# Hybrid attention decoder layer: where the tiles begin in SBUF

## The chip, the cores and the metric

The kernel runs on one NeuronCore of a Trainium2 chip, as one launch. The metric is the device time of that launch in microseconds (us). Three runs of the kernel before took 886.53, 885.81 and 889.96 us; the median is 886.53 us.

## What is computed

One decoder layer for 512 tokens of 1024 channels, in float32. One input projection feeds two causal mixers: a sparse attention of eight heads with three branches (compressed, selected, window) and a gated DeltaNet of four heads in chunks. Their outputs are projected, gated, merged and projected again, then normed; a gated MLP with a short convolution follows. Cut to its frame:

```python
h = x @ w_in                                   # 1024 -> 5408
y_a = nsa_attention(...) @ w_nsa_out           # 512 -> 1024
y_b = gated_deltanet(...) @ w_gdn_out          # 512 -> 1024
mix = (sigmoid(gate_a) * y_a + sigmoid(gate_b) * y_b) @ w_o
x = layer_norm(ALPHA * x + mix, ln1_g, ln1_b)
h = causal_dwconv(x @ ffn_w_up, ffn_conv_w)    # 1024 -> 5632
gate, val = split(h, 2)
f = (silu(gate) * val) @ ffn_w_down            # 2816 -> 1024
x = layer_norm(ALPHA * x + f, ln2_g, ln2_b)
```

## The kernel before

**The products.** Each large product is done in three passes of float32r parts. Both operands are split into a high part (a float32r copy) and a low part (the rest), and `product` (L192) adds high by high, high by low and low by high in one PSUM bank:

```python
PE.matmul(ps, wh[k], mh_(k), start=(k == 0), stop=False)
PE.matmul(ps, wh[k], ml_(k), start=False, stop=False)
PE.matmul(ps, wl[k], mh_(k), start=False, stop=(k == n - 1))
```

The first operand is stationary: 128 columns of it are loaded into TensorE before each matmul (LDWEIGHTS, shown as PEld). The second is moving: 512 columns of it, 2048 bytes of each partition, stream through. A matmul and the weight load of the next one overlap, so both read SBUF at once.

**The stages.** All work is issued through a tile framework that sets the order by priorities (a written-out `ORDER`, with a shift for each step) and the waits by the tiles' places.

- Phase one, up to about 376 us: the token-major projection (`pb`), then the channel-major input projections (`gemm_t` L205, tiles `gps`: weights `wh`/`wl` stationary, `xh`/`xl` moving), interleaved with both mixers. The mixers' own products are small: scores (`aps`), values (`pout` L773: `vcat` stationary, `pth`/`ptl` moving, 256 columns), and many float32 products and transposes (`dps`) of the DeltaNet.
- Merge, about 376 to 464 us (L832 to L872): the outputs are split into `yoh` (high) and `yol` (low); each step does some gate projections (`gps`, as above) and then the mixers' output projections (`pm`: `wh`/`wl` stationary, `yoh`/`yol` moving).
- w_o and the first norm, about 464 to 511 us (L923 to L941, `pw`): here `mh`/`ml` are stationary and `woh`/`wol` move; the normed rows are transposed back into `mh`/`ml`.
- Up product, about 511 to 758 us (L949 to L995, `pu`): `wh`/`wl` stationary, `mh`/`ml` moving; the first two pairs of units run by halves of 256 columns (L958 to L964). The convolution and the gate run beside it on VectorE, ScalarE and GpSimd and write `ah`/`al`.
- Down product, about 758 to 879 us (L1000 to L1027, `pdn`): `ah`/`al` stationary, the streamed `wh`/`wl` moving; the last eight blocks of the second half have their weights kept in tiles of their own, `th`/`tl` (L1012 to L1020), so that each token tile ends in turn. The second norm follows and the rows go out.

**The places.** A pool takes a stretch of each partition's bytes; pools stack from the left end up or from the right end down, and a pool closed gives its stretch to the next one. A tile begins where the tiles before it in its pool end, rounded up to 32 bytes. Nothing else in the program fixes an address. On the left the constants' pool (`cp`, L143) holds 512, 32 and 528 bytes, so the pool `stream` (`wp`, L144: `raw`, `wh`, `wl`, all of 2048 or 4096 bytes) and all that stacks on it (`xh`, `xl`, `yol`, `x1`, `ah`, `al`) begin 192 bytes past a multiple of 256. On the right the stack starts 32 bytes below a multiple of 256, and `mh`, `ml`, `yoh`, `woh`, `wol`, `th`, `tl` begin 224 past one. In phase one the small tiles of `nsa` and `slots` (16 to 384 bytes, L150 and L151) stand among the large ones and shift them.

Of the kernel before, what the change touches and what calls it, by code (L numbers as in the profile page):

```python
# [10 lines left out]
F32 = mybir.dt.float32  # L11
# [119 lines left out]
def body(ctx: ExitStack, tc: tile.TileContext, d, out):  # L131
# [1 line left out]
    V, A, G, PE = nc.vector, nc.scalar, nc.gpsimd, nc.tensor  # L133

    def E(name, h, d="V"):
        """The engine of a step in its h-th turn."""
        return {"V": V, "G": G, "A": A}[ENGINE.get(f"{name}{h}", d)]

    def bc(ap, shape):
        return ap.to_broadcast(shape)  # L140

    psum = lambda name, bufs: ctx.enter_context(tc.tile_pool(name=name, bufs=bufs, space=PSUM))
    cp = ctx.enter_context(tc.tile_pool(name="consts", bufs=1))  # L143
    wp = ctx.enter_context(tc.tile_pool(name="stream", bufs=2))  # L144

    early = ExitStack()
    pool = lambda st, **kw: st.enter_context(tc.tile_pool(**kw))
    xp = pool(early, name="xp", bufs=1, side="left")
    ph1 = ExitStack()
    nsa = pool(ph1, name="nsa", bufs=1, side="right")  # L150
    sp = pool(ph1, name="slots", bufs=1, side="right")  # L151
    def slot(tag, name, shape=(128, 512), dt=F32):
        return sp.tile(list(shape), dt, name=name, tag=tag, bufs=BUFS[tag])

# [5 lines left out]
    dps = lambda shape=(128, 512): pd.tile(list(shape), F32, name="dps")  # L160
    aps = lambda shape=(128, 512): pa.tile(list(shape), F32, name="aps")

    # ---------------------------------------------------------------- loads
    xh = xp.tile([128, KD, S], F32R, name="xh")
    xl = xp.tile([128, KD, S], F32R, name="xl")

# [4 lines left out]
        V.tensor_tensor(xl[:, k, :], xr, xh[:, k, :].bitcast(F32), op=OP.subtract)  # L171

    def split_w(src, shape, eng, first=A):
        """The rows of a unit as two float32r parts, in two halves along its first free dimension."""
        raw = wp.tile(shape, F32, name="raw", bufs=BUFS["raw"])
        nc.sync.dma_start(out=raw, in_=src)
        half = shape[1] // 2
        hi, lo = [], []
        for i in range(2):
            r = raw[:, i * half:(i + 1) * half]  # L180
            wh = wp.tile([128, half] + list(shape[2:]), F32R, name="wh", bufs=BUFS["wh"])
            if first is A:
                A.activation(wh, r, AF.Copy)  # L183
            else:
                first.tensor_copy(wh, r)
            wl = wp.tile([128, half] + list(shape[2:]), F32R, name="wl", bufs=BUFS["wl"])
            eng.tensor_tensor(wl, r, wh.bitcast(F32), op=OP.subtract)  # L187
            hi += [wh[:, k] for k in range(half)]
            lo += [wl[:, k] for k in range(half)]
        return hi, lo  # L190

    def product(ps, w, m, n):  # L192
        """Three passes of float32r parts, w stationary, over n blocks of the contraction."""
        (wh, wl), (mh_, ml_) = w, m
        first = None
        for k in range(n):
            i = PE.matmul(ps, wh[k], mh_(k), start=(k == 0), stop=False)  # L197
            first = first or i
            PE.matmul(ps, wh[k], ml_(k), start=False, stop=False)  # L199
            PE.matmul(ps, wl[k], mh_(k), start=False, stop=(k == n - 1))  # L200
        return first
# [12 lines left out]
    def rsqrt(o, i, n):  # L214
        G.tensor_tensor(o, i, minus_half[:, :n], op=OP.pow)  # L215

    # -------------------------------------------- token-major projections
    vcat = nsa.tile([128, TT, 2, 2, 2, 64], F32R, name="vcat")
    gsig = nsa.tile([128, TT, 24], F32, name="gsig")
    bd = nsa.tile([128, TT, 8], F32, name="bd")  # L220
# [56 lines left out]
    gdt = rows("gdt", d["gdt"], 4)  # L277


    # decay and beta of all heads: [token in chunk, chunk, head]  # L280
    hbeta = nsa.tile([128, TT, GH], F32, name="hbeta")
    beta = nsa.tile([128, TT, GH], F32, name="beta")
    gdec = nsa.tile([128, TT, GH], F32, name="gdec")
# [39 lines left out]
        A.activation(eg.rearrange("p a b c -> p (a b c)"), ps[:, :48], AF.Exp)  # L323
        V.scalar_tensor_tensor(nbe, beta, -1.0, eg[:, 0], op0=OP.mult, op1=OP.mult)

    # ----------------------------------------------------------- GDN
    yo_tile = lambda name, dt=F32: yo.tile([128, S], dt, name=name, tag="yo", bufs=9)
    yT, oT = [None] * GH, [None] * GH

# [34 lines left out]
            e.tensor_tensor(o, i, bc(f, c4), op=OP.mult)  # L364

    def norms(h, i, ps):
        """Reciprocal lengths over the channels of ps: [token, chunk, channel]."""
        ss = sp.tile([128, TT], F32, name="ss", bufs=2)
        rn = sp.tile([128, TT], F32, name=f"rn{i}", bufs=2)
        junk = sp.tile([128, 128], F32, name="junk", bufs=1)  # L370
        for c in range(TT):
            A.activation(junk, ps[:, c, :], AF.Square, accum_out=ss[:, c:c + 1])
        V.tensor_scalar(ss, ss, 4.0 * RMS_EPS, None, op0=OP.add)
        rsqrt(rn, ss, TT)
        return rn
# [65 lines left out]
    def gdn_tri(h):  # L441
        st = HS[h]
        m = st["m"]
        # 16 x 16 diagonal blocks by substitution
        lo = slot("mid", "lo", c4)
        E("lo", h).tensor_tensor(lo, m, bc(C["low"][:, None, :], c4), op=OP.mult)
        f16 = sp.tile([128, TT, 16], F32, name="f16", bufs=2)
# [133 lines left out]
        yT[h] = yo_tile("yT")  # L581
        V.scalar_tensor_tensor(yT[h], py.rearrange("p a b -> p (a b)"), gnw, gs, op0=OP.mult, op1=OP.mult)

    # ----------------------------------------------------------- NSA
    KK = {}

    def keys(g):
        """Keys of one group, of the selected and the window branch, each part twice over the partitions."""
        ps = gemm_t(18 + g, after=HOLD.get("k") if g else None)
        hh_ = nsa.tile([128, 2, S], F32R, name="kh")  # L590
        ll_ = nsa.tile([128, 2, S], F32R, name="kl")
        KK[g] = (hh_, ll_)
        for br in range(2):
            hh, ll = hh_[:, br], ll_[:, br]
            own, oth = slice(br * 64, br * 64 + 64), slice(64 - br * 64, 128 - br * 64)
            for rows_ in (own, oth):
                A.activation(hh[rows_], ps[own], AF.Copy)
            for rows_ in (own, oth):
                V.tensor_tensor(ll[rows_], ps[own], hh[own].bitcast(F32), op=OP.subtract)  # L599
# [113 lines left out]
    POUT = {}  # L713

    def scores(h, u):
        """Exponentials of one or two query tiles, scaled by gate over sum: [query, branch, key]."""
        g = h // 4
        slope = 2.0 ** -(h + 1)
        parts = UNITS[u]
        w = 512 // len(parts)  # L720
        ps = aps((128, len(parts), w))
        s = slot("att", "sc", (128, len(parts), w))
        mn = nsa.tile([128, 3, len(parts)], F32, name="mn", bufs=3)
        br, t = parts[0]
        n = (t + 1) * 128
        brs, ts = slice(br, br + len(parts)), slice(t * 128, n)
        PE.matmul(ps[:, :, :n], Q2[h][:, ts], KK[g][0][:, brs, :n], start=True, stop=False)
        HOLD["k"] = HOLD[h] = PE.matmul(ps[:, :, :n], Q2[h][:, ts], KK[g][1][:, brs, :n], start=False, stop=True)
        for i, (br, t) in enumerate(parts):
            n = (t + 1) * 128  # L730
            V.tensor_tensor_reduce(out=s[:, i, :n], in0=ps[:, i, :n], in1=C["alibi"][:, 512 - n:], scale=-slope,  # L731
                                   scalar=3.0e38, op0=OP.add, op1=OP.min, accum_out=mn[:, 0, i:i + 1])
            A.activation(s[:, i, :n], s[:, i, :n], AF.Exp, scale=-1.0, bias=mn[:, 0, i:i + 1],  # L733
                         accum_out=mn[:, 1, i:i + 1])
        V.reciprocal(mn[:, 2, :], mn[:, 1, :])
        for i, (br, t) in enumerate(parts):
            n = (t + 1) * 128
            e = E(f"p{u}", h)
            sc = gsig[:, t, (br + 1) * 8 + h:(br + 1) * 8 + h + 1]
            if e is A:  # L740
                V.tensor_tensor(mn[:, 2, i:i + 1], mn[:, 2, i:i + 1], sc, op=OP.mult)
                A.activation(s[:, i, :n], s[:, i, :n], AF.Copy, scale=mn[:, 2, i:i + 1])
            else:
                e.tensor_scalar(s[:, i, :n], s[:, i, :n], mn[:, 2, i:i + 1], sc, op0=OP.mult, op1=OP.mult)
        return s

    def flip(h, u, s):
        """Their transposes as two parts, and the products with the values once a half is whole."""
        g = h // 4
        parts = UNITS[u]  # L750
        br, t = parts[0]
# [53 lines left out]
        A.activation(t, ps, AF.Tanh, scale=0.5)  # L805
        MG[i] = t

    # --------------------------------------------------- order of phase one
    pd = ps1.enter_context(tc.tile_pool(name="pd", bufs=BUFS["pd"], space=PSUM))
    pa = ps1.enter_context(tc.tile_pool(name="pa", bufs=BUFS["pa"], space=PSUM))  # L810
    po = ps1.enter_context(tc.tile_pool(name="po", bufs=1, space=PSUM))
# [16 lines left out]
    ph1.close()  # L828
    ps1.close()

    # ------------------------------------------------------------- merge
    mix = ExitStack()  # L832
    mx = pool(mix, name="mx", bufs=1, side="right")
    mh = mx.tile([128, KD, S], F32R, name="mh")
# [39 lines left out]
    early.close()  # L874
    ps2.close()

    # ------------------------------------------------- w_o and first norm
    ln = ctx.enter_context(tc.tile_pool(name="ln", bufs=1, side="left"))
    x1 = ln.tile([128, TT, D], F32, name="x1")
    ln2 = ln.tile([128, 2, D], F32, name="ln2")  # L880
    fs = ctx.enter_context(tc.tile_pool(name="fs", bufs=1, side="left"))
# [8 lines left out]
    rows_of(ln1, 0)  # L890

    def layer_norm(r, gb, st, after=lambda i: None):
        """r: the rows' values, normed in place by halves; st: their two bn_stats."""
        mv = ln.tile([128, 2], F32, name="mv", bufs=2)
        V.bn_aggr(out=mv, in_=st)
        rs = ln.tile([128, 1], F32, name="rs", bufs=2)
        V.tensor_scalar(rs, mv[:, 1:2], LN_EPS, None, op0=OP.add)  # L897
        rsqrt(rs, rs, 1)
        for i in range(2):
            cs = slice(i * 512, (i + 1) * 512)  # L900
            V.scalar_tensor_tensor(r[:, cs], r[:, cs], mv[:, 0:1], gb[:, 0, cs], op0=OP.subtract, op1=OP.mult)
            V.scalar_tensor_tensor(r[:, cs], r[:, cs], rs, gb[:, 1, cs], op0=OP.mult, op1=OP.add)
            after(i)
# [37 lines left out]
        layer_norm(r, ln1, st)  # L941
    wos.close()

    # --------------------------------------------------------------- FFN
    NE = 2
    fws = ExitStack()
    fw = pool(fws, name="fw", bufs=1, side="left")
# [111 lines left out]
```

## Time and profile before

| what | value |
|---|---|
| median of three runs | 886.53 us |
| lowest and highest | 885.81 and 889.96 us |
| span of the profiled execution | 886.6 us |
| TensorE busy (matmul) | 856.7 us, 97% |
| VectorE busy | 563.9 us, 64% |
| ScalarE busy | 384.9 us, 43% |
| GpSimd busy | 159.3 us, 18% |
| bytes moved | 76.33 MB |

The profiled execution's own time stands here as its span, 886.6 us; no time around it is shown. The page counts a matmul as busy from its start to a modelled end, and matmuls overlap, so the busy share does not tell how closely they follow each other. That is read from the timeline, where the first number of a row is the start in us from the beginning of the span.

### The profile page before, as it was taken

What the parts mean: (1) busy time and instruction counts of PE and PEld (TensorE: products, weight loads), DVE (VectorE), ACT (ScalarE), POOL (GpSimd) and SP (SyncE); (2) the same over time, 40 slices, a digit from 0 to 9 for tenths busy, and PEclk for the clock granted to TensorE, in tenths of its full rate; (3) what the DMA queues carried; (4) which work ended last, traced back from release to release, by engine and by line L of the source; (5) the groups of instructions that cost most, each with busy time, mean ns of one, the idle gap of its engine ahead of it and who ended that gap; (6) DMA issues with size and microseconds to landing.
All of it is one profiled execution on the core that took longest, in us unless ns stands there. A gap on an engine that the chain in (4) does not pass through costs nothing.

```text
span 886.6 us, 11725 instructions
## 1 busy us (share of the span) xinstructions
PE 856.7 (97%) x4292; PEld 698.9 (79%) x4292; DVE 563.9 (64%) x1159; ACT 384.9 (43%) x855; POOL 159.3 (18%) x141
## 2 busy tenths in 40 slices
PE   9899799989899899999999999999999999999996
PEld 8677687767787678888888898888888888888885
DVE  5755769985856976585457646666666666423337
ACT  5463267567356666542234114444444444322220
POOL 1232342324334220111100001111111111000001
PEclk9999799999989999999999999999999999999999
DMA  8322111101211010254356002222222222333222
GB/s 265 94 76 91 48 48 36 37 25 48 61 36 48 25 48 25 72 167 152 122 178 237 24 1 72 96 95 94 93 90 93 91 93 93 102 105 97 97 72 95
DMA packets 22954, 76.33 MB, mean 86 GB/s; under 512 B 3184, under 2 KB 3568, under 8 KB 22640
## 3 DMA queue, kind: packets, MB, share of 16 engines
q1 hardware_dynamic: 22896, 75.57, 25.9%
q8 instruction: 34, 0.56, 0.3%
q14 instruction: 24, 0.20, 0.1%
HBM read 73.47 MB, written 2.10 MB: 85 GB/s over the span
## 4 chain that ended last, share of the span: by engine, by line
PE 86%; DVE 9%; ACT 3%; issue 1%; DMA 1%; POOL 0%; SPq 0%; DVEq 0%; ACTq 0%; POOLq 0%
PE pu L200 9%; PE pu L197 9%; PE pu L199 9%; PE gps L197 7%; PE gps L200 7%; PE gps L199 7%; PE pdn L1003 5%; PE pdn L1004 5%; PE pdn L1002 5%; PE pout L773 2%; PE pm L197 2%; DVE tmp L463 2%; PE pm L200 2%; PE pm L199 2%; PE pw L936 2%; PE pw L938 2%
## 5 line engine op out<-in xcount | busy, mean ns | idle before, releaser
L187 DVE TENSOR_TENSOR wl<-raw,wh 128x512 fp32r<-128x512 f32 (+1 forms) x172 | 134.1, 781 | 142.3 <-ACT wh L183 139.3
L183 ACT ACTIVATE wh<-raw 128x512 fp32r<-128x512 f32 (+1 forms) x198 | 122.6, 622 | 234.2 <-PE pu L199 107.5
L197 PE MATMUL pu<-mh,wh 128*128 128x512 f32 (+1 forms) x384 | 144.3, 376 | 0.0
L199 PE MATMUL pu<-ml,wh 128*128 128x512 f32 (+1 forms) x384 | 144.3, 376 | 0.0
L200 PE MATMUL pu<-mh,wl 128*128 128x512 f32 (+1 forms) x384 | 144.3, 376 | 0.0
L197 PE MATMUL gps<-xh,wh 128*128 128x512 f32 x320 | 131.4, 411 | 1.0 <-DVE kl L599 0.6
L200 PE MATMUL gps<-xh,wl 128*128 128x512 f32 x320 | 130.5, 408 | 0.0
L199 PE MATMUL gps<-xl,wh 128*128 128x512 f32 x320 | 129.2, 404 | 0.0
L187 POOL TENSOR_TENSOR wl<-raw,wh 128x512 fp32r<-128x512 f32 x48 | 63.5, 1325 | 171.8 <-ACT wh L183 107.0
L200 PEld LDWEIGHTS pu<-mh,wl 128*128 128x128 f32 x384 | 72.0, 187 | 14.8
L199 PEld LDWEIGHTS pu<-ml,wh 128*128 128x128 f32 x384 | 72.0, 188 | 14.7
L197 PEld LDWEIGHTS pu<-mh,wh 128*128 128x128 f32 x384 | 72.0, 187 | 14.6
L987 DVE SCALAR_TENSOR_TENSOR fa<-pu,fcw,fa 128x511 f32<-128x511 f32 x88 | 65.7, 746 | 10.3 <-ACT fa L984 8.8
L197 PEld LDWEIGHTS gps<-xh,wh 128*128 128x128 f32 x320 | 61.1, 191 | 13.1 <-issue 1.5
L200 PEld LDWEIGHTS gps<-xh,wl 128*128 128x128 f32 x320 | 61.2, 191 | 11.2 <-POOL wl L187 0.3
L199 PEld LDWEIGHTS gps<-xl,wh 128*128 128x128 f32 x320 | 61.2, 191 | 10.6 <-issue 0.4
L993 POOL TENSOR_TENSOR fth<-fth,fa 128x512 f32<-128x512 f32 x22 | 28.7, 1304 | 219.7 <-DVE fa L987 219.7
L1003 PE MATMUL pdn<-wl,ah 128*128 128x512 f32 x144 | 56.0, 389 | 0.0
L1002 PE MATMUL pdn<-wh,ah 128*128 128x512 f32 x144 | 56.0, 389 | 0.0
L1004 PE MATMUL pdn<-wh,al 128*128 128x512 f32 x144 | 56.0, 389 | 0.0
L733 ACT ACTIVATE sc<-sc,mn 128x384 f32<-128x384 f32 (+2 forms) x64 | 35.7, 558 | 15.0 <-DVE mn L731 14.3
L215 POOL TENSOR_TENSOR rs<-rs,minus_half 128x1 f32<-128x1 f32 x8 | 7.5, 941 | 185.7 <-DVE rs L897 185.7
(295 smaller groups left out, 1543.3 us busy)
## 6 DMA issues: line engine op xcount, KB each, us to landing
raw<-in_up SPq DMA_DIRECT2D x44, 512.0 KB, 3.6
raw<-in_wT SPq DMA_DIRECT2D x40, 512.0 KB, 3.6
raw<-in_down SPq DMA_DIRECT2D x22, 512.0 KB, 3.4
raw<-in_wm SPq DMA_DIRECT2D x8, 512.0 KB, 3.6
raw<-in_wo SPq DMA_DIRECT2D x8, 512.0 KB, 3.5
xr<-in_xT SPq DMA_DIRECT2D x8, 256.0 KB, 4.7
ln<-in_lnr SPq DMA_DIRECT2D x2, 1024.0 KB, 6.5
xax<-in_x SPq DMA_DIRECT2D x4, 512.0 KB, 5.2
```

Of the source, the lines that this page charges most:

```text
L183: A.activation(wh, r, AF.Copy)
L187: eng.tensor_tensor(wl, r, wh.bitcast(F32), op=OP.subtract)
L197: i = PE.matmul(ps, wh[k], mh_(k), start=(k == 0), stop=False)
L199: PE.matmul(ps, wh[k], ml_(k), start=False, stop=False)
L200: PE.matmul(ps, wl[k], mh_(k), start=False, stop=(k == n - 1))
L463: V.tensor_tensor(tmp[:, :, :n], lx[:, :, r + 1:, r], bc(xs[:, :, r:r + 1], (128, TT, n)), op=OP.mult)
L733: A.activation(s[:, i, :n], s[:, i, :n], AF.Exp, scale=-1.0, bias=mn[:, 0, i:i + 1], accum_out=mn[:, 1, i:i + 1])
L987: V.scalar_tensor_tensor(acc[:, n:], ps[:, :S - n], w[:, i:i + 1], acc[:, n:], op0=OP.mult, op1=OP.add)
L993: G.tensor_tensor(th, th, g[1], op=OP.mult)
L1002: PE.matmul(ps, ah[:, k, ts], wh, start=(k == 0), stop=False)
L1003: PE.matmul(ps, ah[:, k, ts], wl, start=False, stop=False)
L1004: PE.matmul(ps, al[:, k, ts], wh, start=False, stop=(k == NF - 1))
```

## The change

A helper class `Rows` takes the place of three pools of phase one and of the pool of the norms. It keeps two pools: one for tiles whose bytes in a partition are a multiple of 256, and one (its name ends in `_s`) for all others; at the end it fills the second up to a multiple of 256. At both ends of SBUF a tile of its own (128 bytes left, 224 right) moves the start of the stack to a multiple of 256. All sizes, loops, engines and priorities stay.

```diff
+    class Rows:
+        def __init__(self, st, name, bufs, **kw):
+            self.small = st.enter_context(tc.tile_pool(name=name + "_s", bufs=bufs, **kw))
+            st.callback(self.fill)
+            self.big = st.enter_context(tc.tile_pool(name=name, bufs=bufs, **kw))
+            self.bufs, self.used = bufs, {}
+        def tile(self, shape, dt, name, tag=None, bufs=None):
...
+            n = 4 * math.prod(shape[1:])
+            if n % 256 == 0:
+                return self.big.tile(list(shape), dt, **kw)
+            n, m = -(-n // 32) * 32, bufs or self.bufs
+            self.used[tag or name] = max(n * m, self.used.get(tag or name, 0))
+            return self.small.tile(list(shape), dt, **kw)
+        def fill(self):
+            left = -sum(self.used.values()) % 256
+            if left:
+                self.small.tile([128, left // 4], F32, name="rest")
...
-    cp = ctx.enter_context(tc.tile_pool(name="consts", bufs=1))
+    for side, n in (("left", 128), ("right", 224)):
+        edge = ctx.enter_context(tc.tile_pool(name="edge_" + side, bufs=1, side=side))
+        edge.tile([128, n // 4], F32, name="edge_" + side)
+    cp = Rows(ctx, "consts", 1)
...
-    nsa = pool(ph1, name="nsa", bufs=1, side="right")
-    sp = pool(ph1, name="slots", bufs=1, side="right")
+    nsa = Rows(ph1, "nsa", 1, side="right")
+    sp = Rows(ph1, "slots", 1, side="right")
...
-    ln = ctx.enter_context(tc.tile_pool(name="ln", bufs=1, side="left"))
+    ln = Rows(ctx, "ln", 1, side="left")
```

The rest of the diff takes out comments. Every engine's instructions stand in the same order as before, and their waits are the same but for one: the first copy into `yoh` (L850) no longer waits for GpSimd. What differs is where the tiles begin. The table gives the first byte in the partition and its remainder after division by 256 and by 512, worked out from the pools' sizes:

| tile (role) | before | by 256 | by 512 | now | by 256 | by 512 |
|---|---|---|---|---|---|---|
| `xh` (moving in `gps`) | 42176 | 192 | 192 | 42496 | 0 | 0 |
| `wh`, first slot (streamed weights) | 29888 | 192 | 192 | 30208 | 0 | 0 |
| `yoh` (moving in `pm`) | 106464 | 224 | 480 | 106240 | 0 | 256 |
| `yol`, first (moving in `pm`) | 74944 | 192 | 192 | 75264 | 0 | 0 |
| `mh` (moving in `pu`, stationary in `pw`) | 196576 | 224 | 480 | 196352 | 0 | 256 |
| `woh` (moving in `pw`) | 131040 | 224 | 480 | 130816 | 0 | 256 |
| `ah` (stationary in `pdn`) | 77504 | 192 | 192 | 77824 | 0 | 0 |
| `th`, first (moving in `pdn`) | 196576 | 224 | 480 | 196352 | 0 | 256 |
| `vcat` (stationary in `pout`) | 171520 | 0 | 0 | 171264 | 0 | 256 |
| `pth` (moving in `pout`) | 189440 | 0 | 0 | 182016 | 0 | 256 |

The blocks inside these tiles begin at steps of 512 or 1024 bytes or of a multiple of them.

## Rows read from the trace of the kernel before

**Rows 1.** The page: busy time by engine, and the chain's shares by engine.
```profile
PE 856.7 (97%) x4292; PEld 698.9 (79%) x4292; DVE 563.9 (64%) x1159; ACT 384.9 (43%) x855; POOL 159.3 (18%) x141
...
PE 86%; DVE 9%; ACT 3%; issue 1%; DMA 1%; POOL 0%; SPq 0%; DVEq 0%; ACTq 0%; POOLq 0%
```

**Rows 2.** Busy time by stretch (instructions in brackets), clock, DMA share and rate.
```profile
core 0: us, PE busy (x) PEld busy (x) DVE busy (x) ACT busy (x) POOL busy (x), PEclk, DMA share, GB/s
88.00:110.00 22.00, 16.43 (x83) 13.80 (x82) 15.74 (x36) 5.11 (x10) 7.91 (x7) 0.77 0.15 48
200.00:300.00 100.00, 94.24 (x536) 75.34 (x534) 67.69 (x189) 59.61 (x177) 39.35 (x34) 0.97 0.16 48
376.00:464.00 88.00, 88.00 (x385) 71.80 (x384) 52.57 (x70) 27.20 (x41) 12.77 (x12) 1.00 0.48 156
600.00:700.00 100.00, 100.00 (x431) 80.30 (x430) 67.41 (x90) 42.73 (x72) 11.61 (x9) 1.00 0.29 95
```

**Rows 3.** Timeline of PE across one merge step: start, length, instruction.
```profile
393.15 0.39 PE L197 MATMUL gps<-xh,wh 128*128 128x512 f32 x1
...
404.03 0.40 PE L197 MATMUL pm<-yoh,wh 128*128 128x512 f32 x1
...
409.63 0.39 PE L197 MATMUL gps<-xh,wh 128*128 128x512 f32 x1
```

**Rows 4.** Timeline of PE in the second half of the down product.
```profile
758.56 0.40 PE L1002 MATMUL pdn<-wh,ah 128*128 128x512 f32 x1
...
856.55 0.40 PE L1002 MATMUL pdn<-th,ah 128*128 128x512 f32 x1
...
878.72 0.40 PE L1004 MATMUL pdn<-th,al 128*128 128x512 f32 x1
```

**Rows 5.** Timeline of PE inside the up product.
```profile
619.96 0.40 PE L197 MATMUL pu<-mh,wh 128*128 128x512 f32 x1
...
642.36 0.40 PE L197 MATMUL pu<-mh,wh 128*128 128x512 f32 x1
```

**Rows 6.** Timeline of PE at the start of the w_o product.
```profile
464.66 0.39 PE L936 MATMUL pw<-woh,mh 128*128 128x512 f32 x1
...
481.66 0.39 PE L936 MATMUL pw<-woh,mh 128*128 128x512 f32 x1
```

**Rows 7.** Lines by form: the products of 512 columns, with their counts.
```profile
L197 PE MATMUL gps<-xh,wh 128*128 128x512 f32 x320 | 131.4, 411 | 1.0 <-DVE kl L599 0.6 <-DVE acc L340 0.5
L199 PE MATMUL pu<-ml,wh 128*128 128x512 f32 x320 | 126.4, 395 | 0.0
...
L197 PE MATMUL pm<-yoh,wh 128*128 128x512 f32 x64 | 25.5, 398 | 0.0
...
L1002 PE MATMUL pdn<-th,ah 128*128 128x512 f32 x32 | 12.6, 395 | 0.0
```

**Rows 8.** Timeline of PE: two runs of products of 256 columns.
```profile
163.05 0.28 PE L773 MATMUL pout<-pth,vcat 128*128 128x256 f32 x1
...
164.60 0.28 PE L773 MATMUL pout<-ptl,vcat 128*128 128x256 f32 x1
...
511.28 0.28 PE L197 MATMUL pu<-mh,wh 128*128 128x256 f32 x1
...
516.77 0.28 PE L200 MATMUL pu<-mh,wl 128*128 128x256 f32 x1
```

**Rows 9.** Timeline of PE in phase one: two stretches of input projections.
```profile
33.86 0.63 PE L197 MATMUL gps<-xh,wh 128*128 128x512 f32 x1
...
36.42 0.62 PE L197 MATMUL gps<-xh,wh 128*128 128x512 f32 x1
...
119.80 0.48 PE L197 MATMUL gps<-xh,wh 128*128 128x512 f32 x1
...
124.91 0.39 PE L199 MATMUL gps<-xl,wh 128*128 128x512 f32 x1
```

More of the change, by code (lines that the diff above doesn't have):

```diff
@@ L140, in bc @@
         return ap.to_broadcast(shape)
+    class Rows:
[5 more added lines that the diff above has]
+        def tile(self, shape, dt, name, tag=None, bufs=None):
+            kw = {"name": name}
+            if tag is not None:
+                kw["tag"] = tag
+            if bufs is not None:
+                kw["bufs"] = bufs
+            n = 4 * math.prod(shape[1:])
[8 more added lines that the diff above has]
+                self.small.tile([128, left // 4], F32, name="rest")
     psum = lambda name, bufs: ctx.enter_context(tc.tile_pool(name=name, bufs=bufs, space=PSUM))
-    cp = ctx.enter_context(tc.tile_pool(name="consts", bufs=1))
+    for side, n in (("left", 128), ("right", 224)):
+        edge = ctx.enter_context(tc.tile_pool(name="edge_" + side, bufs=1, side=side))
+        edge.tile([128, n // 4], F32, name="edge_" + side)
+    cp = Rows(ctx, "consts", 1)
     wp = ctx.enter_context(tc.tile_pool(name="stream", bufs=2))
```

## The prediction

> **What bounds the kernel now.** The page comes first: TensorE is busy for 97% of the span, and the chain that ends last runs over it for 86% [rows 1]. VectorE (64%) and ScalarE (43%) have room. The busy time by stretch, read next, shows where TensorE really is the limit: from 376 us on there is no stretch without a matmul in flight, at full clock, while VectorE works 67 of 100 us in the up product [rows 2]. In phase one TensorE has holes (94 of 100 us at 200 to 300, 16.4 of 22 at 88 to 110), and the granted clock falls there (0.77 in the second). So from 376 us to the last product at 878.72 us [rows 4] the time is the number of matmuls times the distance from one start to the next. That distance is not in the grouped lines, whose mean of some 400 ns is a modelled length [rows 7]; it has to be taken from the timeline, as first start, last start and the number of matmuls between.
>
> **What the distances show.** The same matmul, 128x512 in float32r, runs at two paces.
>
> - Merge: 48 products of `gps` take 404.03 - 393.15 = 10.88 us, 226.7 ns each; the next 24, of `pm`, take 409.63 - 404.03 = 5.60 us, 233.3 ns each [rows 3]. The stationary operand comes out of the same slots in both, and the neighbouring engines do the same work; the moving tile differs.
> - Down product: 432 products from streamed `wh`/`wl` take 97.99 us, 226.8 ns each; the 96 from `th`/`tl` that follow take 22.17 us over 95 distances, 233.4 ns each [rows 4]. The stationary tiles are the same; again only the moving tile changes.
> - Up product: 96 distances in 22.40 us, 233.3 ns [rows 5]. w_o: 75 distances in 17.00 us, 226.7 ns [rows 6].
>
> Put beside the table of places: at 226.7 ns moving and stationary operand begin at the same remainder by 256 (`gps` and the first part of `pdn` 192 and 192, `pw` 224 and 224). At 233.3 ns some operand begins 32 bytes off the others (`pu`: 224 against 192; `th`/`ah`: 224 against 192; `pm`: `yoh` 224, `yol` and the weights 192). `pw` is the row to look at: both operands sit at the odd remainder 224, and the pace is still the good one. So it is not a tile's own remainder that costs, but two remainders that differ, and it costs 6.6 to 6.7 ns a matmul. My reading is that the weight load and the moving stream, which read SBUF at once, get in each other's way a little more when their blocks are not cut at the same places.
>
> **The change part by part.** It adds and takes away no instruction that computes or moves data, and moves none on any queue; every term is a change of pace on TensorE. Counts are from the lines by form [rows 7], three passes each.
>
> 1. `pu`, 512 columns: 3 x 320 = 960 products, 233.3 to 226.7: -6.4 us.
> 2. `pm`: 3 x 64 = 192 products: -1.3 us.
> 3. `th`/`tl`: 96 products, 233.4 to 226.8: -0.6 us.
> 4. `pu` by halves, 4 units x 2 halves x 24 = 192 products of 256 columns. With differing remainders they stand 116.8 ns apart (5.49 us over 47 distances); the only run of that shape with equal ones, `pout`, stands 119.2 apart (1.55 us over 13) [rows 8]. So this shape may lose: 192 x 2.4 ns = +0.5 us. I take that, as the only row there is; the other end would be a gain of the same size as the wide ones have by column, 116.8 to half of 226.7, 192 x 3.5 ns = -0.7 us.
> 5. `gps`, `pw` and the first part of `pdn` have equal remainders before and after: 0. So has `pout`.
> 6. Phase one otherwise: its float32 products and transposes are short, and the pairs `kh`/`q2` are equal in both versions. Here nothing in the rows gives a price. A stretch of 23 `gps` products, equal remainders and all, runs at 232.3 ns (5.11 us over 22) [rows 9], since after each interruption by other work the first few stand further apart; the change does not touch the interruptions, so I take 0. If all 768 projections of phase one (960 less four groups of 48 in the merge) gained those 5.6 ns, it would be -4.3 us. On the other side, six distances at the lower of the clock's two levels, 1.2 GHz, take 36.42 - 33.86 = 2.56 us, 1.2 us more than at 2.4 [rows 9]; a shifted schedule may add or lose one such drop or two: up to +2.4 us.
> 7. Transfers: destinations move to multiples of 256 as well. DMA is 1% of the chain [rows 1] and at most 48% busy in the stretches of the rows [rows 2], so even a transfer some per cent shorter is worth under half a microsecond, nearly all of it at the start. Taken as 0.
> 8. The wait dropped at `yoh`'s first copy: GpSimd was not what it waited for last; 0. The places of tiles made no wait longer, as all others are the same.
>
> Sum: -6.4 - 1.3 - 0.6 + 0.5 = -7.8 us. What hides beside TensorE in those stretches still fits: the up product would take 97.1 us where it takes 100, against 67.4 of VectorE and 42.7 of ScalarE [rows 2]. The tail after the last product stays. Against the profiled execution's 886.6 us that gives 878.8; its span is within 0.1 us of the median of the runs, so the same sum stands against the median: **878.7 us**.
>
> **Rivals.**
>
> *The place does nothing.* The two paces could come from something that moves with the tile but is not its remainder by 256: how far apart the operands lie, or the remainder by 512. After the change `mh`, `yoh` and `th` begin 256 off the weights by 512, so in `pu`, `pm` and `th` the operands still differ there, and in the table before every pair that is equal by 256 is equal by 512 too: the rows cannot part these. If the operands must agree by 512, terms 1 to 4 are all void and the time stays at 886.5. Against it speaks that the weight blocks already step by 512 bytes against a fixed moving tile without any change of pace, so the grain of the effect is not coarse, and that 32 bytes are the only difference that a row shows to cost anything. Chance 0.16. The Trainium skill, TensorE: Matmul & The Clock Gate, Step-by-step (in the section on what happens when you issue a matmul), says that TensorE has two independent SBUF read ports and that loading the next weights does not steal bandwidth from the running matmul; by that rule no place of a tile could change a pace, and the change would give nothing. The trace does not agree: 226.7 and 233.3 ns for one shape in one stretch.
>
> *Equal starts at 0 are the bad case.* `pout` is the only run whose tiles begin at remainder 0, and of the two 256-column runs it is the slower, by 2.4 ns [rows 8]. If it is the zero that costs, and by column, every 512-column product would pay 4.8 ns: 2832 of them (960 `gps`, 960 `pu`, 192 `pm`, 192 `pw`, 528 `pdn`), of which the 1248 in terms 1 to 3 gain 6.6 first. That is +13.6 - 8.3 + 0.5, 892.3 us. It decides if `gps` in the merge goes above 230 ns. Against it: what `pout` takes beyond half of a 512-column pace (119.2 - 113.3) need not grow with columns, and nothing sets 0 apart from 192, where the good pace is. Chance 0.04.
>
> *Phase one gains too.* If the spacing after interruptions also came from unequal remainders (float32 tiles at 64 and 128 against `xh` at 192), term 6 gives up to -4.3 us: 874.4. The 5.6 ns are there, but the stretch recovers by itself while its operands stay where they are, which speaks against. Chance 0.08.
>
> **How the numbers follow.** The forecast has 0.72. Its own range, from the ends of terms 4 and 6 with a microsecond for the runs' scatter, is 876 to 882. The range to hold 8 in 10 takes in phase one's gain and most of the case of no effect: 873.5 to 887.0; left out are the slower rival and the far edges. About 0.5% (4.4 us) is what a measurement of this kernel can tell from no change. Faster by more than that, below 882.1: the forecast but for a few hundredths at its upper edge, and phase one's gain, 0.77. Within it: that edge and the case of no effect, 0.19. Slower: 0.04.
>
> **What would show it.** Right, if in the timeline after the change `pm`, `pu` and `th` start 226 to 227 ns apart and `gps`, `pw` and streamed `pdn` stay there; the stretch from the first product of the merge to the last of `pdn` must be about 8 us shorter and phase one as long as before. Wrong in the first way, if `pu` stays at 233; in the second, if `gps` rises. If `pu` does go to 227 and the total does not follow, phase one took it back: its clock and its holes show where.

## The result, and the profile after

| | median (runs) | range | span of the profiled execution |
|---|---|---|---|
| before | 887.61 us (4) | 885.81 to 889.96 | 886.6 |
| after | 878.08 us (4) | 877.23 to 879.48 | 877.7 |

The ratio is 0.9898, with a 95% interval of 0.9869 to 0.9928: faster by about 1%, where 878.7 us was forecast. On another chip six more runs of it, beside eleven of the kernel before, gave 877.73 against 886.02 us, ratio 0.9905 [0.988, 0.9931]. One execution is left out of the medians below, the profiled one of E2: it ran at a granted clock of 0.75 and took 1044.33 us, where all others ran at 0.98 or more.

The page after the change, busy time and chain, answers to [rows 1]:

```profile
PE 847.1 (97%) x4292; PEld 698.2 (80%) x4292; DVE 562.6 (64%) x1159; ACT 384.8 (44%) x855; POOL 159.9 (18%) x141
...
PE 86%; DVE 9%; ACT 2%; issue 1%; DMA 1%; POOL 0%; SPq 0%; DVEq 0%; ACTq 0%; POOLq 0%
```

The counts are those of before, and all the other engines have their old busy time within 1.3 us. Only the matmuls' busy time went down, by 9.6 us, and the chain still runs over TensorE for 86%. So nothing else became the bound; the same work is done at another pace. Busy time by stretch after the change, with the columns of [rows 2]:

```profile
200.00:300.00 100.00, 94.15 (x540) 75.24 (x541) 68.47 (x191) 60.85 (x182) 39.37 (x34) 0.98 0.16 48
376.00:464.00 88.00, 88.00 (x390) 72.88 (x389) 52.49 (x71) 26.71 (x41) 13.05 (x12) 1.00 0.48 157
600.00:700.00 100.00, 100.00 (x443) 82.81 (x442) 69.99 (x93) 44.18 (x73) 12.66 (x10) 1.00 0.31 95
```

From 600 to 700 us 443 matmuls now fall into the stretch where 431 did, with TensorE at 100 of 100 us and full clock both times: the busy share says nothing of the gain, the count says all of it. From 200 to 300 us, in phase one, 540 stand against 536.

The distances, from the timeline of the matmuls after the change (start, length, instruction; the code stands 32 lines further down). One step of the merge, as in [rows 3]:

```profile
391.84 0.39 PE L229 MATMUL gps<-xh,wh 128*128 128x512 f32 x1
...
402.72 0.39 PE L229 MATMUL pm<-yoh,wh 128*128 128x512 f32 x1
...
408.16 0.39 PE L229 MATMUL gps<-xh,wh 128*128 128x512 f32 x1
```

48 products of `gps` in 10.88 us and 24 of `pm` in 5.44: 226.7 ns for both, where `pm` had 233.3. The up product over 96 distances, as in [rows 5], the start of w_o over 75, as in [rows 6], and the down product's streamed part (432) and last part (95 distances), as in [rows 4], which span all of it from its first product:

```profile
619.84 0.39 PE L229 MATMUL pu<-mh,wh 128*128 128x512 f32 x1
...
641.60 0.39 PE L229 MATMUL pu<-mh,wh 128*128 128x512 f32 x1
```

```profile
462.56 0.39 PE L968 MATMUL pw<-woh,mh 128*128 128x512 f32 x1
...
479.56 0.40 PE L968 MATMUL pw<-woh,mh 128*128 128x512 f32 x1
...
750.40 0.39 PE L1034 MATMUL pdn<-wh,ah 128*128 128x512 f32 x1
...
848.35 0.39 PE L1034 MATMUL pdn<-th,ah 128*128 128x512 f32 x1
...
869.88 0.39 PE L1036 MATMUL pdn<-th,al 128*128 128x512 f32 x1
```

21.76 us over 96 is 226.7 ns for `pu` (before 233.3); `pw` stays at 17.00 over 75, 226.7; streamed `pdn` 97.95 over 432, 226.7; `th`/`tl` 21.53 over 95, 226.6 (before 233.4). The runs of 256 columns, as in [rows 8], and the stretch of phase one, as in [rows 9]:

```profile
163.54 0.28 PE L805 MATMUL pout<-pth,vcat 128*128 128x256 f32 x1
...
165.10 0.28 PE L805 MATMUL pout<-ptl,vcat 128*128 128x256 f32 x1
...
508.88 0.28 PE L229 MATMUL pu<-mh,wh 128*128 128x256 f32 x1
...
514.51 0.28 PE L232 MATMUL pu<-mh,wl 128*128 128x256 f32 x1
```

```profile
120.35 0.48 PE L229 MATMUL gps<-xh,wh 128*128 128x512 f32 x1
...
125.45 0.39 PE L231 MATMUL gps<-xl,wh 128*128 128x512 f32 x1
```

`pu` by halves went from 116.8 to 119.8 ns (5.63 us over 47), as feared; `pout` stands at 120.0 (1.56 over 13, where it took 1.55). The stretch of 23 `gps` products of phase one still runs at 231.8 ns (5.10 us over 22).

By stage, from the first product of each to the first of the next (before, after): phase one up to the first `pm` 376.35 and 375.52 us; merge 88.31 and 87.04; w_o 46.62 and 46.32; up product 247.28 and 241.52; down product 120.16 and 119.48; tail 7.88 and 7.83.

### The profile page after: what moved, and what is told of

The parts are those of the page before. It is cut to its first block, busy times and chain, and to the rows that moved or that the text cites. A ratio compares the mean times of both kernels' runs of the same rounds, so it can differ in the third digit from the quotient of the medians.

```text
span 877.7 us, 11725 instructions
## 1 busy us (share of the span) xinstructions
PE 847.1 (97%) x4292; PEld 698.2 (80%) x4292; DVE 562.6 (64%) x1159; ACT 384.8 (44%) x855; POOL 159.9 (18%) x141
## 4 chain that ended last, share of the span: by engine, by line
PE 86%; DVE 9%; ACT 2%; issue 1%; DMA 1%; POOL 0%; SPq 0%; DVEq 0%; ACTq 0%; POOLq 0%
PE pu L229 9%; PE pu L231 9%; PE pu L232 9%; PE gps L229 7%; PE gps L232 7%; PE gps L231 7%; PE pdn L1036 5%; PE pdn L1034 5%; PE pdn L1035 5%; PE pout L805 2%; DVE tmp L495 2%; PE pw L969 2%; PE pw L970 2%; PE pm L232 2%; PE pm L231 2%; PE pw L968 2%
## 5 line engine op out<-in xcount | busy, mean ns | idle before, releaser
L231 PEld LDWEIGHTS pu<-ml,wh 128*128 128x128 f32 x384 | 72.3, 188 | 12.3
L231 PEld LDWEIGHTS gps<-xl,wh 128*128 128x128 f32 x320 | 61.1, 191 | 10.6 <-issue 0.4
```

## The experiments

E1's diff is against the kernel before, all others' against the kernel after. The first five kernels keep the work as it is and move tiles only.

**E1, a single tile of 32 bytes ahead of the left stack** (6 runs, beside 17 of the kernel before). All tiles that the 512-column products read then begin 224 past a multiple of 256, on both sides, and none on a multiple. `vcat` and `pth` lie on the right in phase one and stay where they were, on a multiple.

```diff
+    edge = ctx.enter_context(tc.tile_pool(name="edge", bufs=1))
+    edge.tile([128, 8], F32, name="edge")
```

> The kernel before with one tile of 32 bytes ahead of its left stack: all large tiles of both stacks now begin 224 bytes past a multiple of 256, none on a multiple. Theory (the two operands of a matmul must begin at the same remainder; which remainder does not matter): pm, pu and th/tl go from 233.3 to 226.7 ns a start, gps, pw and streamed pdn stay at 226.7, the 256-column pu goes from 116.8 to 119 to 120; 878 to 880 us in all. Rival 1 (each tile must itself begin on a multiple of 256): pm, pu and th stay at 233 or more, 886 us or more. Rival 2 (the pace depends on how far apart the operands lie, and the pools' order did it): nothing changes, 887 us.

Measured: median 878.79 us against 886.42, ratio 0.9924 [0.9894, 0.9953]. The timeline of its matmuls in one merge step:

```profile
388.40 0.39 PE L199 MATMUL gps<-xh,wh 128*128 128x512 f32 x1
...
399.28 0.39 PE L199 MATMUL pm<-yoh,wh 128*128 128x512 f32 x1
...
404.72 0.39 PE L199 MATMUL gps<-xh,wh 128*128 128x512 f32 x1
```

`gps` 226.7 ns (10.88 over 48), `pm` 226.7 (5.44 over 24); `pu`, `pw` and `th` also 226.7, `pu` by halves 119.85. Merge, up product and down product take 87.04, 241.52 and 119.48 us, to the hundredth what they take after the change. So the whole gain is had without one of these tiles on a multiple of 256. What counts is the remainder of one operand against the other.

**E2, the change with its right stack moved on by 32 bytes** (12 runs, beside the same 17).

```diff
-    for side, n in (("left", 128), ("right", 224)):
+    for side, n in (("left", 128), ("right", 192)):
```

> The changed kernel with the right edge tile of 192 bytes in place of 224: the right stack (yoh, mh, woh, th, pth, vcat) begins 32 bytes past a multiple of 256, everything else of the change stays. Theory: pm, pu and th/tl back at 233.3 ns, 256-column pu at 116.8, gps, pw, pout and streamed pdn as they were; 878.1 + 7.8 = about 886 us. Rival (the gain comes from taking the small tiles out from among the large ones, or from phase one): about 878 us.

Measured: median 885.78 us over eleven runs against 886.42, ratio 0.9991 [0.9967, 1.0015]. The gain is gone, although the left stack, the pools of small tiles and the filling up are all as in the change. Its profile is of the execution with a granted clock of 0.75 (span 1042.5 us); the distances of this right stack at full clock are in the next kernel. The timeline of the down product, first with equal remainders (432 products), then with 32 bytes between them (95 distances), tells something else:

```profile
885.18 0.43 PE L1034 MATMUL pdn<-wh,ah 128*128 128x512 f32 x1
...
1007.74 0.43 PE L1034 MATMUL pdn<-th,ah 128*128 128x512 f32 x1
...
1034.68 0.43 PE L1036 MATMUL pdn<-th,al 128*128 128x512 f32 x1
```

122.56 us over 432 is 283.7 ns, 26.94 over 95 is 283.6. At that clock, in this one execution, the 32 bytes cost nothing that shows. The pace is that of one column a clock, by an estimate 512 / (0.75 x 2.4 GHz) = 284 ns; so is that of the six distances of [rows 9] at 1.2 GHz, 426.7 ns or 512 / 1.2. At full clock the same estimate is 213.3 ns, and equal remainders take 13 ns more, 32 bytes another 6.7. Neither is a fixed addition to each product, then: the 13 ns show at neither lower clock, the 6.7 not at 0.75.

**E2b, the same, and `ah`, `al` begun 8 bytes into their tiles** (one run). E3 and E4 are made with the same helper and other numbers.

```diff
-    for side, n in (("left", 128), ("right", 224)):
+    for side, n in (("left", 128), ("right", 192)):
...
+    def off(p, shape, dt, name, at):
+        n = math.prod(shape[1:])
+        t = p.tile([128, n + 64], dt, name=name)[:, at // 4:at // 4 + n]
+        return t.rearrange("p (a b) -> p a b", a=shape[1])
...
-    ah = fp.tile([128, NF, S], F32R, name="ah")
-    al = fp.tile([128, NF, S], F32R, name="al")
+    ah = off(fp, [128, NF, S], F32R, "ah", 8)
+    al = off(fp, [128, NF, S], F32R, "al", 8)
```

> The run of the right stack at 32 bytes past a multiple of 256, once more for its paces (the profile of the first one fell on a slow execution), with ah/al begun 8 bytes into their tiles besides. Theory: pm and pu at 233.3 ns, th (32 against 8) at about 233; streamed pdn (0 against 8 bytes) at about 232 if two words cost as one word did, 226.7 if 8 bytes are as free as 16 were for most of that stage. 886 us, and up to 2.5 us more from streamed pdn.

Measured: 891.61 us. The timeline of one merge step:

```profile
394.62 0.39 PE L235 MATMUL gps<-xh,wh 128*128 128x512 f32 x1
...
405.49 0.40 PE L235 MATMUL pm<-yoh,wh 128*128 128x512 f32 x1
...
411.10 0.39 PE L235 MATMUL gps<-xh,wh 128*128 128x512 f32 x1
```

`pm` is back at 233.8 ns over the step (5.61 over 24; 233.4 within it) and `gps` at 226.5, as in [rows 3]. `pu` has 233.3 again and, by halves, 116.7. Merge and up product take 88.31 and 247.28 us, to the hundredth what they took before the change. Streamed `pdn`, 8 bytes apart, loses its good pace: 230.7 ns, and `th` 231.1.

**E3 and E4, other differences** (one run each): right stack 64 bytes on and `ah`, `al` 16 (E3); 128 and 4 (E4).

> The changed kernel with the right stack 64 bytes past a multiple of 256 and ah/al (stationary in pdn) begun 16 bytes into their tiles. Which remainder counts: if that by 64, pm and pu stay at 226.7 ns; if that by 128 or 256, they go to about 233. The streamed pdn has operands 16 bytes apart: about 233 if any difference below 64 costs, 226.7 if only steps of 32 do; th against ah is 48 apart: about 233 in either case. If all differ, about +8 us for pm, pu, th and +2.9 us for streamed pdn.

> The changed kernel with the right stack 128 bytes past a multiple of 256 and ah/al begun 4 bytes into their tiles. If the remainder by 64 or by 128 counts, pm and pu stay at 226.7 ns; if that by 256, they go to about 233. The streamed pdn has operands one word apart: about 233 if any difference costs, 226.7 if a difference within 16 or 32 bytes is free.

Measured: 883.74 and 888.69 us. At 64 bytes `pu` takes 228.9 ns and, by halves, 117.8; at 128 bytes 233.3 and about 119 to 120. So neither the remainder by 64 nor that by 128 is the one that counts, and 64 bytes cost `pu` a third of what 32 do. `pm`, in which one product of three (the one with `yol`) has equal remainders, goes the other way: 233.2 and 228.9; why was not found out. `th`, 48 bytes from `ah` in E3, takes 231.9, where about 233 was expected; in E4, 124 bytes from it, it settles at 226.7 after six products. Streamed `pdn` takes 232.4 at 4 bytes. At 16 bytes it has both paces in one run, as the timeline of E3 shows (48 distances each):

```profile
764.00 0.39 PE L1040 MATMUL pdn<-wh,ah 128*128 128x512 f32 x1
...
774.88 0.39 PE L1040 MATMUL pdn<-wh,ah 128*128 128x512 f32 x1
...
818.50 0.39 PE L1040 MATMUL pdn<-wh,ah 128*128 128x512 f32 x1
...
829.70 0.39 PE L1040 MATMUL pdn<-wh,ah 128*128 128x512 f32 x1
```

10.88 us, 226.7 ns each, and then 11.20 us, 233.3. The operands and their places are of one kind throughout. From the 273rd of the 528 products on, shortly after the second half begins, some distances are 228 to 236 ns in the kernel after, too; there the pace is back at 226.7 after six of them, and in E3 it stays at 233.3.

**E5 to E7, the pace measured by itself** (one run each). Behind one part of phase one the kernel also does series of 36 products into a PSUM tile that nobody reads; these are additional work, and the kernels' own times mean nothing. The moving blocks lie in `xh`, the stationary ones in `xl`, begun `mo` and `so` floats into their tiles. The line of E5; E6 and E7 have other lists and, where told, another step or width:

```diff
+    for mo, so, cols, rows_ in [(0, 0, 512, 128), (1, 0, 512, 128), ...
+        for i in range(36):
+            PE.matmul(idle[:rows_, :cols], fl[:, so + 128 * (i % 12):so + 128 * (i % 12) + rows_],
+                      fx[:, mo + 512 * (i % 6):mo + 512 * (i % 6) + cols], start=True, stop=True)
```

> The changed kernel with 16 series of 36 products of its own, put in after the token-major projection: stationary 128 columns out of xl, moving 512 columns out of xh, weight blocks stepping by 512 bytes and moving blocks by 2048, into a PSUM bank that nobody reads. Between the series only the moving operand's start differs: 0, 4, 8, 16, 32, 48, 64, 96, 128, 160, 192, 224, 256 and 512 bytes past the stationary one's remainder, then the stationary one 32 bytes on, then 0 again. Theory (a remainder that differs by 256 costs): 226.7 ns at 0, 256 and 512, more at all others but perhaps 4 to 16, and the same at moving +32 and stationary +32. Rival (only some differences cost, as 64, 96 or 128 do in one stage and not in another): paces that do not follow the difference alone. About 576 products of 0.23 us, 133 us, on top of the changed kernel's time.

> The changed kernel with 14 series of 36 products, as in the run beside it, now with other sizes: 128, 64 and 32 stationary columns at equal starts; 64 columns at 32 bytes of difference; both operands at +32 and both at +100; 256 moving columns at 0, 32, 64 and 128 bytes; 384 columns at 0 and 32; 128 columns at 0; the first again. Theory (the excess over the columns' own time is the weight load and the moving stream hindering each other): with 64 stationary columns the excess of 13 ns at equal starts falls to half or less and that at 32 bytes from 20 to about 10; both at +32 and both at +100 as at 0. Rival (a fixed price of a matmul, whatever is loaded): 226.7 with 64 and 32 columns too. 256 columns: about 119 to 120 at equal starts, 117 at 32 bytes, as in the two runs of the kernel. About 100 us on top.

> The changed kernel with 13 series of 36 products of 512 columns, as in the other two runs of that kind: equal starts; stationary +16; moving +32; stationary +16 again; then with the weight block fixed (no step) at 0 and at 32 bytes; with both blocks fixed at 0 and at 32; with one moving column repeated 512 times (step 0) at 0 and at 32; moving +128 against stationary +4; weight blocks stepping by 544 and by 768 bytes. Theory (pace depends on how the two streams fall into step, and a stream once in step stays so): stationary +16 runs at 226.7 when it follows equal starts and at 233 when it follows +32; fixed blocks as stepping ones, 226.7 and 233.3; steps of 544 bytes cost, steps of 768 do not. If the 13.3 ns over 213.3 come from reading the moving columns, the repeated column drops below 220 and loses its dependence on the 32 bytes; if they are a price of the weight load, it stays at 226.7. Rival (the place alone sets the pace): stationary +16 has one pace whatever ran before.

In the timeline a steady piece of a series is one row: start, length, and the number of products at the end. The length less that of one product, over the distances, is the pace. E5, with the moving blocks 0, 32, 64 and 256 bytes on, and last the stationary ones 32 bytes on:

```profile
21.20 6.07 PE L288 MATMUL gps<-xh,xl 128*128 128x512 f32 x26
...
54.67 6.23 PE L288 MATMUL gps<-xh,xl 128*128 128x512 f32 x26
...
71.33 6.12 PE L288 MATMUL gps<-xh,xl 128*128 128x512 f32 x26
...
121.59 6.05 PE L288 MATMUL gps<-xh,xl 128*128 128x512 f32 x26
...
137.98 6.23 PE L288 MATMUL gps<-xh,xl 128*128 128x512 f32 x26
```

(6.07 - 0.39) / 25 is 227 ns at 0, then 234, 229, 226 and 234. Over the last 24 distances of each series, and so a little finer:

| moving begins after stationary by (bytes) | pace, ns |
|---|---|
| 0, 256, 512 | 226.7 |
| 64 | 228.9 |
| 48 | 230.0 |
| 16 | 231.7 |
| 32, 96, 128, 192, 224 | 233.3 |
| 8 | 233.5 |
| 160 | 234.5 |
| 4 | 235.5 |

Each difference was run once, from small to large, so what ran before is not varied here; E7 varies it.

E6: stationary blocks of 64 and of 32 columns at equal starts; both operands 32 bytes on; both 100 bytes on:

```profile
29.27 6.14 PE L288 MATMUL gps<-xh,xl 128*64 128x512 f32 x26
...
37.56 6.18 PE L288 MATMUL gps<-xh,xl 128*32 128x512 f32 x26
...
54.23 6.05 PE L288 MATMUL gps<-xh,xl 128*128 128x512 f32 x26
...
62.51 6.36 PE L288 MATMUL gps<-xh,xl 128*128 128x512 f32 x26
```

Over the last 24 distances that is 230.0, 231.7, 226.7 and 238.3 ns; 64 stationary columns with 32 bytes between the operands give 230.8. The weight loads do get shorter in the trace, 188, 134 and 109 ns for 128, 64 and 32 columns, but a product did not get cheaper, so the extra time does not grow with the loaded columns. Next, 256 moving columns at equal starts and at 64 bytes, and 128 moving columns at equal starts:

```profile
69.90 3.41 PE L288 MATMUL gps<-xh,xl 128*128 128x256 f32 x27
...
78.38 3.22 PE L288 MATMUL gps<-xh,xl 128*128 128x256 f32 x27
...
99.15 3.18 PE L288 MATMUL gps<-xh,xl 128*128 128x128 f32 x27
```

With 256 moving columns the paces are 120.1, 116.7, 113.3 and 118.7 ns at 0, 32, 64 and 128 bytes: at this width equal starts are the worst of the four. With 384 columns 0 and 32 bytes both give 173.3. And 128 columns take 111.7 ns, hardly less than 256, so at 256 the number of columns no longer sets the pace alone.

E7: stationary blocks 16 bytes on, right behind the series at 0; the moving blocks 32 on; stationary 16 on once more, now behind that one; and a single moving column repeated 512 times, at 0 and at 32:

```profile
28.75 6.06 PE L291 MATMUL gps<-xh,xl 128*128 128x512 f32 x26
...
36.97 6.23 PE L291 MATMUL gps<-xh,xl 128*128 128x512 f32 x26
...
45.37 6.23 PE L291 MATMUL gps<-xh,xl 128*128 128x512 f32 x26
...
86.79 5.78 PE L291 MATMUL gps<-xh,xl 128*128 128x512 f32 x26
...
94.56 5.78 PE L291 MATMUL gps<-xh,xl 128*128 128x512 f32 x26
```

Paces: 226.7, 233.3, 233.3, and 215.8 for both with the repeated column. The first and the third are the same products at the same places; they differ in what ran before them. With one and the same weight block loaded anew each time the pace is 226.7 at 0 and 233.3 at 32, as with changing blocks, and so it is with the moving block fixed too. With the moving blocks 128 bytes on and the stationary ones 4 it is 226.7 once more, and with stationary blocks 544 bytes apart 232.8. The last series of each of the three kernels mixes with the kernel's own products after some 13 of its products; until then E7's, with weight blocks 768 bytes apart, runs at 226.7 (12 distances).

**E8, the 256-column shape at its best distance** (6 runs, beside 6 of the kernel after as it is). `vcat` and the weights of the halves begin 192 bytes into tiles 256 bytes longer, so that the moving blocks stand 64 past them.

```diff
-    vcat = nsa.tile([128, TT, 2, 2, 2, 64], F32R, name="vcat")
+    vcat = nsa.tile([128, 8 * 256 + 64], F32R, name="vcat")[:, 48:48 + 8 * 256].rearrange("p (t a b c d) -> p t a b c d", t=TT, a=2, b=2, c=2)
...
-            wh = fw.tile([128, KD, 128], F32R, name=f"wh{p}{b}")
-            wl = fw.tile([128, KD, 128], F32R, name=f"wl{p}{b}")
+            wh = fw.tile([128, KD * 128 + 64], F32R, name=f"wh{p}{b}")[:, 48:48 + KD * 128].rearrange("p (a b) -> p a b", a=KD)
+            wl = fw.tile([128, KD * 128 + 64], F32R, name=f"wl{p}{b}")[:, 48:48 + KD * 128].rearrange("p (a b) -> p a b", a=KD)
```

> The changed kernel with two stationary tiles of the 256-column products moved so that the moving operand begins 64 bytes past the stationary one's remainder by 256: the weights of the first two pairs of the up product (wh00 to wl11) and vcat begin 192 bytes into tiles 256 bytes longer. In the series 256 columns ran at 113.3 ns at that difference and at 120.1 at equal starts. Theory: the up product's halves go from 119.9 to about 113.3 (192 x 6.5 ns = -1.25 us) and pout from about 119 to 113 where it runs without a break (up to -1 us, less where phase one waits for other engines); 876 to 877 us. Rival (weight blocks used for two products in a row fall into step in another way): 117 to 120 and no change, 878.

> The changed kernel itself, as it stands, beside the run with two tiles moved by 192 bytes on the same chip: 877 to 879 us, the ratio to the kernel before 0.988 to 0.992.

Measured: 879.83 us, ratio to before 0.9916 [0.9891, 0.9942], beside 877.73 and 0.9905 [0.988, 0.9931] for the kernel after. `pu` by halves takes 117.8 ns, not the 113.3 of the series, and 119.9 beside it; `pout` 118 against 120. That is 192 x 2.1 ns = 0.4 us, and the up product is that much shorter, 241.15 against 241.52 us. It is a third of the gain that was expected there and less than the medians can tell: they go the other way, within the scatter of their runs. No kernel here is shown to be faster than the change.

## Why the prediction was right, point by point

**The reading of the paces held.** The forecast rested on `pm`, `pu` and `th` being 32 bytes off their weights [rows 3 to 5] and on `pw` having a good pace at an odd remainder [rows 6]. E1 and E2 are the two sides of it: 32 bytes put in without the rest of the change bring the gain (0.9924), and 32 bytes added to the change take it away (0.9991). The price is that of 32 bytes, though, and not of every difference: 64 bytes cost `pu` 2.2 ns (E3), and 124 cost `th` nothing once it had settled (E4).

**The terms**, against the stages:

| term | forecast, us | measured, us |
|---|---|---|
| 1 and 4, up product | -6.4 + 0.5 = -5.9 | 241.52 - 247.28 = -5.76 |
| 2, merge | -1.3 | 87.04 - 88.31 = -1.27 |
| 3, down product | -0.6 | 119.48 - 120.16 = -0.68 |
| 5, w_o | 0 | 46.32 - 46.62 = -0.30 |
| 6, phase one | 0 | 375.52 - 376.35 = -0.83 |
| 7 and 8 | 0 | 0: in E1 the weights arrive 224 past a multiple of 256 and the wait at `yoh` is still there, with the same stages |

From the first `pm` to the last `pdn` that is 494.36 against 502.37 us: -8.0, "about 8 us" as forecast. The medians differ by 9.5 us in the first set and by 8.3 in the second; that 878.08 lies so near 878.7 is in part luck, since the kernel before had a median of 887.61 beside it. Term 4 was taken from one row of another product and came out within 0.7 ns (119.85 for 119.2); with its other end the up product would have lost 7.1.

Phase one's -0.83 us isn't a gain of the change that the runs could show: the first `pm` starts at 373.86 us in the second profile of the same kernel, at 372.08 in E1, 377.81 in E2b and 376.85 in E8. These kernels place some tiles of phase one differently, so the 6 us are not scatter alone; but one and the same kernel is 1.7 us apart in its two profiles, and 17 executions of the kernel before range from 882.90 to 893.27 us.

**The rivals.** *The place does nothing* falls twice: in the kernel after `mh`, `yoh` and `th` are 256 off the weights by 512 and run at 226.7, and E5 gives 226.7 at 256. *Equal starts at 0 are the bad case* falls with `gps`, which stayed at 226.7 in the merge, now at 0. For 256 columns the rival's row was a true one, but it is not the zero that is slower there: in E1 the halves of `pu`, both operands at 224, take the same 119.85 ns. It does not carry over to 512. *Phase one gains too* asked for the stretch of [rows 9] to lose its 5.6 ns; it lost 0.5. Its 4.3 us on top of the 8.0 of the stages would be 12.3, and the intervals of the two sets end at 11.6 and 10.6 us.

**What was wrong is the reason offered**, that the weight load and the moving stream "get in each other's way a little more when their blocks are not cut at the same places". It changed no number of the forecast, but E6 and E7 cut it down. If the load took time from the stream by its amount, 64 or 32 columns should cost less, and they cost more (230.0 and 231.7). Equal cuts are not enough either: both operands at 100 bytes give 238.3. At a granted clock of 0.75 the cost is not there at all (E2). And the load alone costs nothing to see: with the moving column repeated, and the weights loaded as always, 32 bytes make no difference and even the pace of equal starts loses 10.8 ns (226.7 to 215.8). So it takes the moving stream's walk over its columns, and how that walk stands to the loads, since moving either operand by 32 bytes costs and moving both does not (E5, E6). At 16 bytes the stream can hold either of two paces (E7, E3). Where the two reads meet was not found out and stays open; no series ran without weight loads.

## What to carry to other kernels

Where TensorE is busy without a gap, read the distance from start to start, product by product, and put the operands' first bytes beside it: two paces of one shape are time to be had, here 1% for the 32 bytes of one tile. Let moving and stationary tiles of 512-column products begin at the same remainder by 256, on a multiple of 32; that both begin at 0 is not needed. Check other widths by themselves, since 256 columns went the other way here, and other types too, since only float32r was run. Judge such a small gain by its stage, since phase one alone differed by 6 us between these profiles.

## What the hardware showed that was not expected

- The same float32r product of 512 columns took from 215.8 to 238.3 ns at full clock, by the places and steps of its operands alone. The Trainium skill, TensorE: Matmul & The Clock Gate, Back-to-back issue gap, gives N/2.4 + 2.5 ns, which is 215.8 at 512 columns, for the isolated product. Only the repeated column agrees with that (215.8); no stream that reads 512 different columns came below 226.7 here.
- At a granted clock of 0.75 all of this was gone: 283.7 ns with equal remainders and 283.6 with 32 bytes between them, in one down product (E2).
- At 16 bytes the pace depends on what ran before: 226.7 behind the series at 0, 233.3 behind the one at 32, and in E3 a short disturbance changed it for the rest of the product.
- Equal remainders are enough for the good pace at 512 columns, on multiples of 32, but not the only way to it: with 128 bytes against 4 it was 226.7 in E7, and in E4 `th`, at the same remainders, fell to 226.7 too. Why that pair is good was not found out.
- For 256 columns the order of the places is another: 120.1 ns at 0, 118.7 at 128, 116.7 at 32, 113.3 at 64. In the kernel (E8) the place at 64 gave 117.8 only. In `pu` each block of `wh` serves two products in a row, which these series did not do; whether that is the reason was not tried.
